# Batched matmul, fp32 in and out: eleven output stores move from GpSimd's software queue to SyncE's hardware queue

## The chip, the cores and the metric

The kernel runs on one core of a Trainium2 chip. The metric is the device time of one launch in microseconds (us). Before the change the median of three runs is 511.96 us (511.52 to 512.17).

## The reference

```python
x:      (32, 512, 1024)  float32
weight: (32, 1024, 768)  float32
out = np.matmul(x, weight).astype(np.float32)      # (32, 512, 768)
```

Inputs are read once (167.77 MB) and the output is written once (50.33 MB). The two operands are cast from fp32 to bf16 on their way into SBUF; products are summed in fp32.

## The kernel before

**Tiling.** The 32 batches are worked on as 16 pairs (`PAIRS`), numbered 0 to 15; pair k holds batches 2k and 2k+1. A pair's x is one transfer (4.19 MB of fp32), its weights are one transfer of 6.29 MB for pairs 2 to 14, and two of 3.15 MB for pairs 0, 1 and 15 (`together`). Its output is one store of 3.15 MB, except for pair 15, whose batches 30 and 31 are stored separately, 1.57 MB each. Output of a pair is collected in a slot of `outs`.

**Buffers.** There are places for the weights of two pairs (`W_SLOTS` 4 batches), for the x of two pairs (`X_SLOTS` 2) and for the output of four pairs (`OUT_SLOTS` 4). Pair a and pair a+4 share an output slot, so the first copy into it for pair a+4 waits for the store of pair a (`slot_free`, on ACT). Pair 15 uses the slot of pair 11.

**Work on a pair.** TensorE (PE) transposes the pair's x in fp32 words (line 173, tile `pt`); VectorE (DVE) spreads each transposed block into `xT` (lines 219, 227). Then PE multiplies: per batch four blocks of rows (`mt`), each with 8 steps over K and two column ranges (lines 165 and 138, tile `pm`). There are two sets of PSUM tiles; each takes two row blocks, then ACT (lines 261, 265) and DVE (lines 270, 272) copy it to `outs`. DVE does the spreading of pair k+1 before its last copy of pair k, so a pair is copied out shortly after the transposes of the next one.

**Loads.** All loads but one are issued by GpSimd (POOL) on its software queue, q0, in program order. The x of pair k+2 waits until the first products of pair k are done (`load_x`, line 111); the weights of pair k+2 wait until pair k is done (`load_w`, line 98; line 102 for single batches). Only the first half of the first x comes over SyncE's queue.

**Stores before.** POOL issues the stores of pairs 0 to 13 on the same queue q0 (`store`, line 119), two at a time in every second turn of its loop, between the load of x and the load of weights; those of pairs 11, 12 and 13 follow all loads. A store waits until the pair is copied out (`copied`). SyncE (SP) passes on the landings of loads to PE (`landed`, signals `s_xr` and `s_wr`), and at its end issues the store of pair 14 and the two of pair 15 on its hardware queue, q1.

Of the kernel before, what the change touches and what calls it, by code (L numbers as in the profile page):

```python
# [12 lines left out]
def kernel(  # L13
# [7 lines left out]
    B, M, K = x.shape  # L21
# [8 lines left out]
    PAIRS = B // 2  # L30
    HELD = 2
    GROUPS = 2 * MT
    W_SLOTS, X_SLOTS, OUT_SLOTS = 4, 2, 4

    pe, dve, act, pool, sp = nc.tensor, nc.vector, nc.scalar, nc.gpsimd, nc.sync
# [25 lines left out]
    def sem(name):  # L61
        sems.append(nc.alloc_semaphore(name))
        return sems[-1]
# [6 lines left out]
    s_free = sem("s_free")  # L70
    s_a, s_ap, s_d, s_dp = sem("s_a"), sem("s_ap"), sem("s_d"), sem("s_dp")
    s_st = [sem(f"s_st{i}") for i in range(OUT_SLOTS)]
    s_fin = sem("s_fin")


# [14 lines left out]
    def together(b):  # L90
        return W_SLOTS <= b < B - 2

    def load_w(b):
        if together(b):
            if b % 2 == 0:
                pool.wait_ge(s_mm, mm_done(b + 1 - W_SLOTS))
                slots = all_ws[:, b // 2 % 2].rearrange("p r ko n -> p r (ko n)")
                pool.dma_start(out=slots, in_=w_two_view[b // 2]).then_inc(s_w[b % W_SLOTS], 16)  # L98
            return
        if b >= W_SLOTS:  # L100
            pool.wait_ge(s_mm, mm_done(b - W_SLOTS))
        pool.dma_start(out=ws[b % W_SLOTS], in_=w_view[b]).then_inc(s_w[b % W_SLOTS], 16)  # L102

    def loads_of_w(b):

        return sum(not (together(i) and i % 2) for i in range(b % W_SLOTS, b + 1, W_SLOTS))

    def load_x(k):
        if k >= X_SLOTS:
            pool.wait_ge(s_mm, mm_begun(k - X_SLOTS))  # L110
        pool.dma_start(out=xs[k % X_SLOTS], in_=x_view[k]).then_inc(s_x[k % X_SLOTS], 16)  # L111

    def copied(eng, j):
        eng.wait_ge(s_ap, j + 1)
        eng.wait_ge(s_dp, j + 1)

    def store(eng, a, sem):
        copied(eng, 4 * a + 3)
        eng.dma_start(out=two_view[a], in_=outs[a % OUT_SLOTS]).then_inc(sem, 16)  # L119

    def store_one(b):
        copied(sp, 2 * b + 1)
        sp.dma_start(out=one_view[b], in_=last_out(b)).then_inc(s_fin, 16)
# [211 lines left out]
    def landed(eng, slot, n, ready, uses=1):  # L335

        eng.wait_ge(slot, 16 * n).then_inc(ready, uses)

    def on_pool():
        pool.dma_start(out=xs[0][:, MT:], in_=x_view[0, :, MT:]).then_inc(s_rest, 16)  # L340
        load_w(0)
        pool.memset(ident, 0.0).then_inc(s_zero, 1)  # L342
        pool.wait_ge(s_zero, 1)
        pool.affine_select(  # L344
            out=ident,
            in_=ident,
            compare_op=mybir.AluOpType.not_equal,
            fill=1.0,
            base=0,
            pattern=[[-1, P]],  # L350
            channel_multiplier=1,
        ).then_inc(s_ident, 1)
        load_w(1)
        load_x(1)
        load_w(2)
        load_w(3)
        def stores(first, last):
            for a in range(max(first, 0), last):
                store(pool, a, s_st[a % OUT_SLOTS])


        for k in range(PAIRS - 2):
            load_x(k + 2)
            if k % 2 == 0:
                stores(k - 3, k - 1)
            load_w(2 * k + 4)
            load_w(2 * k + 5)
        stores(PAIRS - 3 - HELD, PAIRS - 2)

    def on_sp():  # L370
        for b in range(B):
            if b == 0:
                sp.wait_ge(s_cast, 2).then_inc(s_xr, 1)
            elif b % 2 == 0:
                k = b // 2
                landed(sp, s_x[k % X_SLOTS], (k + 1) // X_SLOTS, s_xr)
            if not (together(b) and b % 2):
                landed(sp, s_w[b % W_SLOTS], loads_of_w(b), s_wr, 1 + together(b))
        store(sp, PAIRS - 2, s_fin)
        store_one(B - 2)  # L380
        store_one(B - 1)
        sp.sem_inc(s_zero, 1)

    def clear_on_pool():

        for i, s in enumerate(s_st):
            pool.wait_ge(s, 16 * len(range(i, PAIRS - 2, OUT_SLOTS)))
        pool.wait_ge(s_zero, 2)
        used = range(sems[0].num, s_fin.num)
        pool.dma_reset(used)  # L390
        pool.sem_clear(used)
        pool.wait_ge(s_fin, 48).then_inc(s_fin, -48)

    sp.dma_start(x_first, x_view[0, :, :MT])
    with tc.tile_critical(sync_engine=mybir.EngineType.Activation, no_gpsimd_drain=True):  # L395
        on_pool()
        tc.wait_critical_data_deps()
        on_pe()
        on_dve()
        on_act()  # L400
        on_sp()
        clear_on_pool()
# [30 lines left out]
```

## Time and profile before

| | |
|---|---|
| Median of 3 runs | 511.96 us |
| Span of the profiled execution | 509.6 us |
| Its own time beside the span | not listed apart; the median stands 2.4 us over this span |
| PE busy | 429.4 us (84%) |
| DVE, ACT, POOL busy | 211.7, 114.1, 29.6 us |
| Queue q0 (POOL's, software) | 126.88 MB at the SBUF side, 96.8% of the time of 16 engines |
| Queue q1 (SP's, hardware) | 8.39 MB, 4.0% |
| Mean granted PE clock | 0.947 |

How to read the lines below. A row of a group or a wait names engine, line and operation, then output <- input by the program's names. In the waits, "A <- B: 103.4, 6, 19.2" says that A waited for B for 103.4 us in 6 times, at most 19.2. In a timeline the first two numbers are start and duration in us from the start of the span, and a bracket gives the idle time before and what ended it. In a table of stretches the columns are: the stretch, its length, busy time and count of PE, PEld (weight loads into PE), DVE, ACT and POOL, the granted PE clock, the busy share of the 16 DMA engines, and GB/s. GB/s and MB of a queue count the SBUF side, where a loaded value has 2 bytes and a stored one 4.

### The profile page before, as it was taken

To read this page: it belongs to the slowest core of one execution; us is meant where nothing else is said; L and a number is where in the kernel's file an instruction comes from. 1 tells how busy PE (TensorE), PEld (TensorE's weight loads), DVE (VectorE), ACT (ScalarE), POOL (GpSimd) and SP (SyncE) were. 2 spreads that over 40 slices of the span, in tenths; PEclk is the share of its full clock that TensorE was granted. 3 is DMA by queue.
4 is the path that set the end of the run, shared out by engine and by line. 5 is a ranking of instruction groups with operands and counts; after the bars stand their busy time and mean duration, and the time that the engine had idled before them with its cause. 6 is when DMAs were issued, how large, how long until landed. Compare 5 with 4: busy or idle time off the path is not lost. (4 is left out here: it accounts for less than half of the span.)

```text
span 509.6 us, 5832 instructions
## 1 busy us (share of the span) xinstructions
PE 429.4 (84%) x2560; PEld 172.8 (34%) x1536; DVE 211.7 (42%) x330; ACT 114.1 (22%) x195; POOL 29.6 (6%) x55
## 2 busy tenths in 40 slices
PE   0899989999899399993999949999399994999990
PEld 0525342443325034250343513434034341433420
DVE  1436362454635136351373514635146351454631
ACT  1131312223130231302313023230231302223230
POOL 3000000000101001010010100100001000100000
PEclk9999998999999799996999979999699997999996
DMA  8999999999999999999999999999999999999998
GB/s 262 216 211 216 225 207 221 215 305 247 221 212 230 432 234 214 217 237 432 226 215 217 247 433 216 218 217 259 420 217 217 219 267 408 218 215 229 432 430 347
DMA packets 9299, 135.29 MB, mean 266 GB/s; under 512 B 848, under 2 KB 848, under 8 KB 848
## 3 DMA queue, kind: packets, MB, share of 16 engines
q0 software_dynamic: 8720, 126.88, 96.8%
q1 hardware_dynamic: 576, 8.39, 4.0%
q14 instruction: 3, 0.02, 0.0%
HBM read 167.77 MB, written 50.33 MB: 428 GB/s over the span
## 5 line engine op out<-in xcount | busy, mean ns | idle before, releaser
L165 PE MATMUL pm<-w,xT 128*128 x1024 | 346.2, 389 | 42.0 <-DVE outs L270 38.7
L138 PE MATMUL pm<-w,xT 128*128 x1024 | 284.7, 278 | 0.0
L165 PEld LDWEIGHTS pm<-w,xT 128*128 128x128 bf16 x1024 | 102.3, 100 | 282.8 <-issue 241.0
L270 DVE COPY outs<-pm 64x512 f32<-64x512 f32 x128 | 88.2, 689 | 207.7 <-DVEq L268 206.3
L261 ACT COPY outs<-pm 64x512 f32<-64x512 f32 x128 | 74.2, 580 | 272.6 <-PE pm L138 168.4
L173 PE MATMUL pt<-ident,x 128*128 128x128 f32 x512 | 84.5, 307 | 24.8 <-PEq L177 14.5
L219 DVE COPY xT<-pt 128x1024 bf16<-128x1024 bf16 x120 | 77.7, 687 | 63.9 <-PE pt L173 63.6
L173 PEld LDWEIGHTS pt<-ident,x 128*128 128x128 f32 x512 | 71.2, 210 | 40.0 <-DVE xT L219 18.8
L265 ACT COPY outs<-pm 64x512 f32<-64x512 f32 x64 | 37.0, 579 | 99.5 <-PE pm L138 99.3
L272 DVE COPY outs<-pm 64x512 f32<-64x512 f32 x64 | 43.9, 686 | 0.0
L98 POOL DMA_DIRECT2D w<-in_weight_dram x13 | 9.2, 708 | 264.6 <-PE pm L138 264.6
L111 POOL DMA_DIRECT2D x<-in_x_dram x15 | 8.4, 557 | 123.2 <-PE pm L138 92.4
L119 POOL DMA_DIRECT2D out_dram<-outs x14 | 7.5, 539 | 7.1 <-DVE outs L272 7.1
L227 DVE COPY xT<-pt 128x512 bf16<-128x512 bf16 x16 | 5.7, 418 | 4.1 <-PE pt L173 4.1
L280 DVE CAST x<-outs 128x1024 bf16<-128x1024 f32 x2 | 1.3, 692 | 11.0 <-DMA outs<-in_x_dram 11.0
L102 POOL DMA_DIRECT2D w<-in_weight_dram x6 | 3.2, 544 | 26.5 <-PE pm L138 26.3
L280 ACT ACT_TABLE_LOAD x1 | 1.3, 1283 | 10.7 <-DMA outs<-in_x_dram 10.7
L280 ACT CAST x<-outs 128x1024 bf16<-128x1024 f32 x2 | 2.0, 1042 | 0.0
L340 POOL DMA_DIRECT2D x<-in_x_dram x1 | 0.7, 670 | 0.8 <-POOLq L417 0.8
L344 POOL TENSOR_SCALAR_AFFINE_SELECT ident<-ident 128x128 f32<-128x128 f32 x1 | 0.3, 284 | 0.2 <-POOL ident L342 0.2
L342 POOL MEMSET ident<- 128x128 f32 x1 | 0.2, 232 | 0.0
L417 POOL MEMSET const-float32-0.0<- 128x1 f32 x1 | 0.1, 99 | 0.2 <-issue 0.2
(3 smaller groups left out, 0.3 us busy)
## 6 DMA issues: line engine op xcount, KB each, us to landing
out_dram<-outs POOLq DMA_DIRECT2D x14, 3072.0 KB, 40.1
w<-in_weight_dram POOLq DMA_DIRECT2D x13, 3072.0 KB, 32.9
x<-in_x_dram POOLq DMA_DIRECT2D x15, 2048.0 KB, 34.3
w<-in_weight_dram POOLq DMA_DIRECT2D x6, 1536.0 KB, 30.5
out_dram<-outs SPq DMA_DIRECT2D x1, 3072.0 KB, 18.7
out_dram<-outs SPq DMA_DIRECT2D x2, 1536.0 KB, 13.6
outs<-in_x_dram SPq DMA_DIRECT2D x1, 2048.0 KB, 9.7
x<-in_x_dram POOLq DMA_DIRECT2D x1, 1024.0 KB, 11.6
```

Of the source, the lines that this page charges most:

```text
L98: pool.dma_start(out=slots, in_=w_two_view[b // 2]).then_inc(s_w[b % W_SLOTS], 16)
L111: pool.dma_start(out=xs[k % X_SLOTS], in_=x_view[k]).then_inc(s_x[k % X_SLOTS], 16)
L119: eng.dma_start(out=two_view[a], in_=outs[a % OUT_SLOTS]).then_inc(sem, 16)
L138: return pe.add_instruction(mybir.InstMatmult(name=nc.get_next_instruction_name(), engine=mybir.EngineType.PE, ins=[pe.lower_ap(moving), p ...
L165: last = pe.matmul(*args, start=(ko == 0), stop=(ko == KT - 1))
L173: last = pe.transpose(pts[g % 2][:, j, :], words[:, mo, j::JT], ident)
L219: return dve.tensor_copy(both[g // 2][:, :, :, g % 2].rearrange("p b j i r -> p j b i r"), pt)
L227: last = dve.tensor_copy(rows, pt[:, :, b])
L261: last = act.copy(*piece)
L265: act.copy(*pieces(b, p, 2)[0]).then_inc(s_ap, 1)
L270: last = dve.tensor_copy(*piece)
L272: dve.tensor_copy(*pieces(b, p, 2)[1]).then_inc(s_dp, 1)
```

## The change

SP issues the stores of pairs 0 to 10 inside its loop over batches: after the weights of pair a+1 have landed and been passed on, it waits for pair a's copies and issues its store on q1. The store of pair 11 is issued by SP when batch 30's weights have landed. The stores of pairs 12 and 13 stay with POOL after all loads, each with a semaphore of its own, and the waits at the very end follow.

```diff
+    s_late, s_last = sem("s_late"), sem("s_last")
...
-        def stores(first, last):
-            for a in range(max(first, 0), last):
-                store(pool, a, s_st[a % OUT_SLOTS])
-
-
         for k in range(PAIRS - 2):
             load_x(k + 2)
-            if k % 2 == 0:
-                stores(k - 3, k - 1)
             load_w(2 * k + 4)
             load_w(2 * k + 5)
-        stores(PAIRS - 3 - HELD, PAIRS - 2)
+        store(pool, PAIRS - 4, s_late)
+        store(pool, PAIRS - 3, s_last)
 
     def on_sp():
+        late = PAIRS - 3 - HELD
         for b in range(B):
...
                 landed(sp, s_w[b % W_SLOTS], loads_of_w(b), s_wr, 1 + together(b))
+            if b % 2 and 2 < b < 2 * late + 2:
+                store(sp, b // 2 - 1, s_st[(b // 2 - 1) % OUT_SLOTS])
+            elif b == B - 2:
+                store(sp, late, s_st[late % OUT_SLOTS])
         store(sp, PAIRS - 2, s_fin)
...
-            pool.wait_ge(s, 16 * len(range(i, PAIRS - 2, OUT_SLOTS)))
+            pool.wait_ge(s, 16 * len(range(i, PAIRS - 4, OUT_SLOTS)))
+        pool.wait_ge(s_late, 16)
+        pool.wait_ge(s_last, 16)
```

## Prediction

> **What bounds the kernel now.** I read the queue totals of the page first, then the waits, then the clock and transfer rate by stretch, then the starts of the last pairs on the PE in order of time.
>
> ```profile
> PE 429.4 (84%) x2560; PEld 172.8 (34%) x1536; DVE 211.7 (42%) x330; ACT 114.1 (22%) x195; POOL 29.6 (6%) x55
> q0 software_dynamic: 8720, 126.88, 96.8%
> HBM read 167.77 MB, written 50.33 MB: 428 GB/s over the span
> ACT outs L261 <- DMA out_dram<-outs: 103.4, 6, 19.2
> PE pm L165 <- DVE outs L270: 38.7, 5, 8.2
> 230.00:240.00 10.00, 1.98 (x7) 0.41 (x3) 1.98 (x3) 2.81 (x5) 0.00 (x0) 0.68 1.00 433
> 270.00:280.00 10.00, 10.00 (x63) 3.04 (x31) 3.97 (x6) 3.47 (x6) 0.00 (x0) 1.00 1.02 217
> ```
>
> The kernel moves 167.77 MB in and 50.33 MB out, and POOL's queue alone keeps the 16 engines busy for 96.8% of the span. The two stretches give the rates. While stores run, 433 GB/s; while loads run, 217 GB/s as counted in bf16 at the SBUF side, which is 434 GB/s of fp32 read. Both kinds cost the same per fp32 byte, and the transfers are what bounds the whole. The waits tell something else: ACT waits six times for a store to empty a slot of `outs`, and the PE behind it loses 38.7 us in five stalls. It is tempting to count those 38.7 us as the gain, because early stores remove that wait. But in the stretch 230 to 240, where the PE is busy for 1.98 us of 10, the transfers run at 1.00. The PE stalls cost nothing at the end as long as the queues never run dry.
>
> So I need the rate over a whole cycle, and then the one place where the PE does matter: the last pairs.
>
> ```profile
> 238.35 0.59 PE L165 MATMUL pm<-w,xT 128*128 x1 [8.02 <-DVE outs L270]
> 301.57 0.58 PE L165 MATMUL pm<-w,xT 128*128 x1 [7.27 <-DVE outs L270]
> 364.63 0.58 PE L165 MATMUL pm<-w,xT 128*128 x1 [7.99 <-DVE outs L270]
> 427.80 0.59 PE L165 MATMUL pm<-w,xT 128*128 x1 [7.22 <-DVE outs L270]
> 426.06 1.17 ACT L261 COPY outs<-pm 64x512 f32<-64x512 f32 x2 [18.26 <-DMA out_dram<-outs]
> 386.13 0.39 PE L165 MATMUL pm<-w,xT 128*128 x1
> 406.94 0.52 PE L173 MATMUL pt<-ident,x 128*128 128x128 f32 x3
> 412.62 0.38 PE L165 MATMUL pm<-w,xT 128*128 x1
> 448.45 0.39 PE L165 MATMUL pm<-w,xT 128*128 x1
> 475.20 0.38 PE L165 MATMUL pm<-w,xT 128*128 x1
> ```
>
> The first four rows end the same stall of pairs 7, 9, 11 and 13, so two pairs take (427.80 - 238.35) / 3 = 63.15 us. A pair moves 4.19 MB of x, 6.29 MB of weights and 3.15 MB of output, 13.63 MB; two pairs in 63.15 us are 431.7 GB/s. One pair costs the transfers 31.57 us, of which a store is 7.29 us and the loads 24.3 us. The other rows start pairs 12, 13, 14 and 15 at 386.13, 412.62, 448.45 and 475.20, with the transposes of pair 13 at 406.94. An undisturbed pair thus takes the PE 20.8 us of products and 26.49 us from start to start (26.75 us into the last). The PE needs 26.5 us where the transfers need 31.6 us with a store and 24.3 us without one.
>
> **The change part by part.** Eleven stores leave POOL's queue for SyncE's.
>
> On SyncE (SP), before: the one early load, then stores of pair 14 and of the last two batches.
>
> ```order
> L394 DMA outs<-in_x_dram 128x4096
> L428 UNCONDITIONAL_BRANCH [waits DMAHW0_49,Activation_sequencer_49]
> L119 DMA out_dram<-outs 128x6144 [waits s_cast,s_w0,s_w1,s_x1,s_w2,s_w3,s_x0,s_dp,s_ap]
> L123 DMA out_dram<-outs 128x3072 [waits s_dp,s_ap] x2
> L395 UNCONDITIONAL_BRANCH
> ```
>
> After, the end of SP's list: stores of pairs 9, 10, 11, 14, then the last two batches (s_x and s_w are landings of x and weights, s_dp and s_ap the copies out).
>
> ```order
> L120 DMA out_dram<-outs 128x6144 [waits s_x0,s_w0,s_dp,s_ap]
> L120 DMA out_dram<-outs 128x6144 [waits s_x1,s_w2,s_dp,s_ap]
> L120 DMA out_dram<-outs 128x6144 [waits s_x0,s_w0,s_x1,s_w2,s_dp,s_ap]
> L120 DMA out_dram<-outs 128x6144 [waits s_w3,s_dp,s_ap]
> L124 DMA out_dram<-outs 128x3072 [waits s_dp,s_ap] x2
> L397 UNCONDITIONAL_BRANCH
> ```
>
> A store of pair a now stands behind the landing of pair a+1's weights and behind its own copies. On POOL before, from the x of pair 13 on:
>
> ```order
> L111 DMA x1<-in_x_dram 128x8192 [waits s_mm]
> L98 DMA w<-in_weight_dram 128x2x6144 [waits s_mm]
> L111 DMA x0<-in_x_dram 128x8192 [waits s_mm]
> L119 DMA out_0_dram<-outs 128x6144 [waits s_dp,s_ap] x2
> L98 DMA w<-in_weight_dram 128x2x6144 [waits s_mm]
> L111 DMA x1<-in_x_dram 128x8192 [waits s_mm]
> L102 DMA w<-in_weight_dram 128x6144 [waits s_mm] x2
> L119 DMA out_0_dram<-outs 128x6144 [waits s_dp,s_ap] x3
> ```
>
> And after, from the same x on:
>
> ```order
> L112 DMA x1<-in_x_dram 128x8192 [waits s_mm]
> L99 DMA w<-in_weight_dram 128x2x6144 [waits s_mm]
> L112 DMA x0<-in_x_dram 128x8192 [waits s_mm]
> L99 DMA w<-in_weight_dram 128x2x6144 [waits s_mm]
> L112 DMA x1<-in_x_dram 128x8192 [waits s_mm]
> L103 DMA w<-in_weight_dram 128x6144 [waits s_mm] x2
> L120 DMA out_0_dram<-outs 128x6144 [waits s_dp,s_ap] x2
> ```
>
> The two stores between x and weights of pair 14 are gone from there, and no load waits in a queue behind a store any more.
>
> *The stalls for slots.* All five go: store a is issued near the landing of pair a+1's weights and its slot is wanted three pairs later. Late next is the weight load. Loads and a store run side by side and share the engines, so a pair's weights come every 31.57 us, and the PE waits for each of them. Nothing of the 38.7 us is gained; it is spread over the pairs. POOL's issues (about half a microsecond each) were hidden and stay so. SP's eleven new waits hold back only SP's next signals, for loads that land later than the store they wait beside (x of the pair after next); price nothing.
>
> *The last four pairs.* Before, by the slot wait that ended at 426.06, the queue had moved x of 15 pairs, weights of 14 and 10 stores, 182.4 MB. After, pair 12 can start when x of 13 pairs, weights of 13 and all 11 early stores are through: 170.9 MB. That is 11.5 MB less, 26.7 us at 431.7 GB/s, so pair 12 starts at 399.4. From there no store runs until pair 11's, loads need 24.3 us a pair, and the PE runs free: pairs 13, 14 and 15 start 26.49, 26.49 and 26.75 us apart, at 479.1 for pair 15 against 475.20 now. Batch 30's weights land near 399.4 + 2 x 24.3 + 9.7 + 7.3 = 465; the store of pair 11, issued then beside the last weights, is down 14.6 us and a fixed part later, about 482. The first copy that needs its slot is due a quarter of 20.8 us after pair 15's start, so that wait costs nothing.
>
> *The clock.* The price of waiting for weights shows in pairs with a stall:
>
> ```profile
> 70.00:80.00 10.00, 7.72 (x37) 4.30 (x31) 6.54 (x11) 0.00 (x0) 0.00 (x0) 0.83 0.97 207
> 76.31 0.39 PE L165 MATMUL pm<-w,xT 128*128 x1 [1.75 <-PEq L177]
> 98.79 1.12 PE L173 MATMUL pt<-ident,x 128*128 128x128 f32 x8
> 132.61 0.39 PE L165 MATMUL pm<-w,xT 128*128 x1 [1.50 <-PEq L177]
> 153.42 0.76 PE L173 MATMUL pt<-ident,x 128*128 128x128 f32 x5
> 222.36 0.38 PE L165 MATMUL pm<-w,xT 128*128 x1
> 254.03 0.65 PE L173 MATMUL pt<-ident,x 128*128 128x128 f32 x4
> ```
>
> After a gap of 1.75 us pair 2 takes 22.48 us (granted clock 0.83 in that stretch), 1.7 us over 20.8. After 1.50 us pair 4 takes 20.81, nothing over. Pair 7, with 8.02 us of stall inside, takes 31.67 - 8.02 = 23.65, so 2.8 us over. In the changed kernel pair 12 starts after a wait of 31.57 - 26.49 = 5.1 us, or 3.1 us if pair 11 itself started slow. Bounds 0 and 2.8; I take 2.0, between the two stalled rows and nearer the shorter gap. For pairs 2 to 11 it is hidden in the wait. For pair 12 it isn't, since nothing behind it waits for loads. Pair 15 then starts at 481.1, 5.9 us later than now.
>
> The Trainium skill, "TensorE: Matmul & The Clock Gate", in the table of why this matters, asks for no idle gap over about 3 us between bursts of matmuls; it speaks against this change. The 1.75 us row shows a slower clock already below that.
>
> *The end.*
>
> ```profile
> 0.74 0.38 SPq L394 DMA_DIRECT2D outs<-in_x_dram  x1
> x<-in_x_dram POOLq DMA_DIRECT2D x1, 1024.0 KB, 11.6
> 1.26 0.67 POOL L340 DMA_DIRECT2D x<-in_x_dram  x1 [0.81 <-POOLq L417]
> 488.04 10.72 SPq L123 DMA_DIRECT2D out_dram<-outs  x2
> DMA to landing us min/median/max: 10.2/37.0/51.8
> ```
>
> The last store is now issued near 488.04 + 10.72 - 0.33 = 498.4 and, as the shortest of all, lands 10.2 us later at 508.6, with others still in flight beside it. After: issued at 498.4 + 5.9 = 504.3, with the rest nearly done. Alone it moves 1.57 MB in 3.6 us plus a fixed part. The first two loads bound that part: both together are 4.19 MB, 9.7 us, and are down at 1.26 + 11.6 = 12.9, which leaves 12.9 - 9.7 - 0.74 = 2.4 us. It lands at 510.4, 1.8 us later than before. The span goes from 509.6 to 511.4; the median of the runs shown, 511.96, stands 2.4 us over the span, which I keep: **513.8 us**. All the transfers alone would end where they do now, so this is a gap at the end in which only the last store runs.
>
> **The rivals.**
>
> *Mixed traffic is slower.* The trace has no stretch in which stores of one queue run beside loads of the other. Eleven stores, each shared for 14.6 us, are 160 us; 1% off the rate there delays pair 12 and so the end by 1.6 us. The lowest rate seen with both queues at work is here:
>
> ```profile
> 490.00:500.00 10.00, 6.16 (x38) 1.76 (x18) 3.97 (x6) 2.32 (x4) 0.00 (x0) 0.99 0.98 421
> ```
>
> Against 433 that is 2.8%, 4.5 us on top: 518.3 us. For it: nothing has shown such a mixture at full rate. Against: the cycle of 63.15 us, with four changes of direction, already reaches 431.7. The other bound is a gain of 0.3%, the 433 of stores alone, 0.5 us.
>
> *Pair 12 starts at full clock.* If its wait falls so that the clock is not lowered, pair 15 starts at 479.1, the last store is issued at 502.3 and would land at 508.4; the transfers together still end at 508.6, so 512.0 us, the same. For it: 1.50 us cost nothing. Against: 1.75 us did. By the skill's rule above, pairs would alternate: a full-clock pair leaves 5.1 us of wait, the next, slow, leaves 3.1 us, about at its limit.
>
> *Faster.* Loads no longer stand behind stores and two queues feed each engine; if that lifts the mixed rate above 431.7 GB/s, pair 12 and the total come 1.6 us earlier per 1%. With pair 12 at full clock this decides from 0.7% on; at 1.5% it gives 509.6 us. Against: stores alone and loads alone both stop at 433 to 434, as if at one limit. The Trainium skill, "DMA: Bandwidth & Descriptors", rules for kernel authors, says spreading transfers over issuing engines does not help, as they interleave on the same 16 engines; no run here shows it yet.
>
> **How the numbers follow.** A run of this kernel can be told from no change from about 0.2%, 1.0 us. Forecast, slower by about 2 us: 0.46. Mixed traffic slower: 0.27. Full clock at pair 12, same: 0.18. Faster: 0.09. Slower together 0.73. The range runs from 511.2, which leaves out the faster cases, to 518.5, the lowest mixed rate seen.
>
> **What would show it.** Right: no ACT wait for stores, PE waits of 3 to 5 us before pairs 2 to 12, clock below 1 after them, pair 12 starting near 399 and pair 15 near 481, the last store landing alone in about 6 us. Wrong: pair 12 starting after 401 (the rate), PE stalls in pairs 13 to 15 (loads issued too late), a span under 508.6, or a rate in the shared stretches clearly off 432.

## The result and the profile after

The changed kernel takes 513.98 us (513.38 to 514.30, 5 runs) against 511.60 us (511.34 to 512.17, 5 runs) on the same chip: a ratio of 1.0042, 95% interval 1.0031 to 1.0053. By that ratio it is slower by 2.1 us (1.6 to 2.7); the two medians lie 2.4 us apart. The forecast was 513.8 us.

Totals and queues of the profile's page after, the PE's waits for weights, and one stretch of 210 us from the table of stretches, first after, then before:

```profile
PE 430.9 (84%) x2512; PEld 174.6 (34%) x1536; DVE 211.6 (41%) x330; ACT 114.4 (22%) x195; POOL 23.1 (5%) x43
q0 software_dynamic: 6992, 89.13, 79.1%
q1 hardware_dynamic: 2304, 46.14, 21.3%
HBM read 167.77 MB, written 50.33 MB: 426 GB/s over the span
PE pm L139 <- PEq L178: 41.6, 9, 9.8
PE pm L139 <- DVE outs L271: 4.5, 2, 2.3
190.00:400.00 210.00, 178.41 (x1036) 72.94 (x638) 89.63 (x137) 45.64 (x79) 8.26 (x13) 0.93 1.01 265
```

```profile
190.00:400.00 210.00, 182.00 (x1079) 73.38 (x651) 89.71 (x137) 46.14 (x81) 13.14 (x22) 0.93 1.02 261
```

No wait of ACT for a store is left in the waits after; it was 103.4 us. In its place stand nine waits of the PE for a signal of SP (`PEq L178`), 41.6 us, about what the five stalls had cost. Two more, 4.5 us together, stand before pairs 5 and 9, put down to the DVE; with them the PE waits before each of pairs 2 to 12. The longest, 9.8 us, is that of pair 2, whose weights land at 84.0 us where they landed at 75.9. The busy share of the DMA engines hardly moves: 1.01 where it was 1.02.

Starts on the PE after, in order of time: products of pairs 6, 10, 11 and 12, the transposes behind pair 12, and products of pairs 13, 14 and 15.

```profile
211.17 0.42 PE L139 MATMUL pm<-w,xT 128*128 x1 [5.31 <-PEq L178]
337.39 0.42 PE L139 MATMUL pm<-w,xT 128*128 x1 [5.30 <-PEq L178]
369.26 0.42 PE L139 MATMUL pm<-w,xT 128*128 x1 [3.52 <-PEq L178]
400.82 0.42 PE L139 MATMUL pm<-w,xT 128*128 x1 [3.77 <-PEq L178]
424.03 0.52 PE L174 MATMUL pt<-ident,x 128*128 128x128 f32 x3
429.92 0.27 PE L139 MATMUL pm<-w,xT 128*128 x1
456.55 0.27 PE L139 MATMUL pm<-w,xT 128*128 x1 [0.20 <-DVE xT L220]
483.29 0.27 PE L139 MATMUL pm<-w,xT 128*128 x1
```

In this trace the very first product of a pair is often missing, so the row shown is the second. The two stand 0.22 us apart at full clock (386.13 and 386.35 before) and 0.40 us at half clock (400.48 and 400.88 in the run `s11pool_again` below), so a start is that much ahead of the row and the wait in its bracket that much shorter. Four pairs take 337.39 - 211.17 = 126.22 us, 31.56 us each. Pair 12, at half clock, starts near 400.4, where it started at 386.13 before; behind it nothing waits, and pair 15 starts at 483.1, where it was 475.20.

Stores after, their first and last issue and the shortest way from issue to landing (the tile `out_dram`), and the last stretch; then the last stretch before:

```profile
L124 SPq DMA_DIRECT2D out_dram<-outs x2: 332/332/332, 495.9 to 506.3; - x2
DMA to landing us min/median/max: 5.1/19.6/40.3
500.00:512.30 12.30, 4.04 (x26) 1.08 (x11) 3.01 (x5) 1.74 (x3) 0.00 (x0) 0.85 0.64 272
```

```profile
500.00:509.60 9.60, 0.00 (x0) 0.00 (x0) 0.00 (x0) 0.00 (x0) 0.00 (x0) 0.50 0.77 326
```

The last store is issued at 506.3 instead of 498.4 and lands 5.1 us later, at 511.4 instead of 508.6. The DMA engines are busy for 0.64 of the time from 500 on, where it was 0.77 before, and the PE still works there for 4.04 us, where it had ended before: too little is left to move beside the last store.

### The profile page after: what moved, and what is told of

Same layout as the page of the kernel before. It is cut to its first block, busy times and chain, and to the rows that moved or that the text cites. A ratio compares the mean times of both kernels' runs of the same rounds, so it can differ in the third digit from the quotient of the medians.

```text
span 512.3 us, 5785 instructions
## 1 busy us (share of the span) xinstructions
PE 430.9 (84%) x2512; PEld 174.6 (34%) x1536; DVE 211.6 (41%) x330; ACT 114.4 (22%) x195; POOL 23.1 (5%) x43
## 5 line engine op out<-in xcount | busy, mean ns | idle before, releaser
L166 PE MATMUL pm<-w,xT 128*128 x976 | 336.6, 394 | 0.0
L139 PE MATMUL pm<-w,xT 128*128 x1024 | 288.0, 281 | 48.3 <-PEq L178 41.6
L120 POOL DMA_DIRECT2D out_dram<-outs x2 | 1.1, 536 | 7.7 <-DVE outs L273 7.6
```

The lines of the kernel that those rows point to most:

```text
L139: return pe.add_instruction(mybir.InstMatmult(name=nc.get_next_instruction_name(), engine=mybir.EngineType.PE, ins=[pe.lower_ap(moving), p ...
L166: last = pe.matmul(*args, start=(ko == 0), stop=(ko == KT - 1))
```

## The experiments

Each kernel was compared with runs of the kernel before on its own chip; the ratio is to those. Theory: early stores stand ahead of pair 12's weights, the PE therefore starts its last four pairs late, and with the lowered clock at pair 12 it ends behind the transfers. Rivals: loads and stores mixed from two queues are slower; the even spacing itself costs; the place of pair 11's store costs.

**Stores two pairs later** (`later2`), the mixture kept:

```diff
-            if b % 2 and 2 < b < 2 * late + 2:
-                store(sp, b // 2 - 1, s_st[(b // 2 - 1) % OUT_SLOTS])
+            if b % 2 and 2 + 2 * 2 < b < 2 * late + 2 + 2 * 2:
+                store(sp, b // 2 - 1 - 2, s_st[(b // 2 - 1 - 2) % OUT_SLOTS])
```

> The changed kernel, with each of the stores of pairs 0 to 10 issued by SyncE two pairs later (pair a's when the weights of pair a+3 have landed); queue, mixture with loads, pair 11's store and the end are as in the changed kernel. Theory (the early stores stand ahead of pair 12's weights, so the PE starts its last four pairs too late and ends last): two stores of 7.3 us fewer before pair 12, which starts near 385 instead of 401; time back to the kernel before, 511.6 us within 0.5. Rival (stores of the hardware queue beside loads of the software queue run slower): as many stores are mixed, so the time stays near 514.

Measured 512.31 us against 511.83, ratio 1.0010 (1.0000 to 1.0019). Pairs 12 and 15 on the PE, and the stores:

```profile
385.69 0.38 PE L139 MATMUL pm<-w,xT 128*128 x1 [3.45 <-PEq L178]
478.20 0.27 PE L139 MATMUL pm<-w,xT 128*128 x1
L124 SPq DMA_DIRECT2D out_dram<-outs x2: 332/332/333, 490.8 to 501.2; - x2
DMA to landing us min/median/max: 8.1/19.6/55.0
```

As many stores are mixed with loads, the PE waits and its clock drops as often, and most of the loss is gone. What counts is which transfers stand ahead of pair 12.

**Stores one pair later** (`later1`): the same edit with `2 * 1` for `2 * 2` and `- 1 - 1` for `- 1 - 2`.

> The changed kernel with each of the stores of pairs 0 to 10 one pair later. Theory: ten early stores instead of eleven stand ahead of pair 12, which starts near 393.5; it waits for pair 13's weights again, so the gain at pair 15 is about 2 us (481), the last store is issued near 503.5 and the transfers end as late as it does: 512.3 us within 0.5, like two pairs later. If each pair earlier costs the same (a rate, not an end), the time is midway between 512.3 and 514.0 or above.

512.26 us against 511.67, ratio 1.0008 (0.9999 to 1.0016): the same as two pairs later, as expected, so the loss is not a fixed amount per pair; it has a point from which it begins.

**One store per turn on the software queue** (`pool1`, `pool1_again`), the kernel before with:

```diff
-            if k % 2 == 0:
-                stores(k - 3, k - 1)
+            stores(k - 2, min(k, PAIRS - 4) - 1)
```

> The kernel before, with its stores of pairs 0 to 10 one in every turn of POOL's loop (pair a in turn a+2) instead of two in every second turn: all on the software queue, nothing mixed, but spread evenly like those of the changed kernel. Theory: pair 12 starts near 385 after nine stores, the PE waits about 5 us for weights in each pair and runs at a lower clock after it, and the end does not move: 511.6 us within 0.5. Rival (the even spacing, with a wait and a lower clock in every pair, is what costs): near 514.

> One store in every turn on the software queue, once more. In its first profile pair 15 started at 478.6 and the last store was issued at 501.7, early enough, and yet all landings at the end came 2 us late, with 3 us between the first and the last of the 16 engines for one load (1 us before). If that spread is of this order of stores on one queue, both the time near 513.7 and the spread return; if it was of that chip or that run, the time goes to 512.

513.70 us against 511.83, ratio 1.0041 (1.0028 to 1.0055); again 513.89 against 511.67, 1.0040 (1.0026 to 1.0053). The expectation of 511.6 us failed here. In the first profile, pairs 12 and 15 and the stores:

```profile
386.97 0.42 PE L138 MATMUL pm<-w,xT 128*128 x1 [3.49 <-PEq L177]
478.64 0.27 PE L138 MATMUL pm<-w,xT 128*128 x1
L123 SPq DMA_DIRECT2D out_dram<-outs x2: 332/332/333, 491.3 to 501.7; - x2
DMA to landing us min/median/max: 8.9/43.1/53.7
```

The PE is early enough, as in `later2`, and yet the last store, issued at 501.7, lands at 510.6. What differs shows in the 16 increments that each transfer makes as its engines finish. For batch 30's weights, first and last engine in us from the start of the span:

```
before        463.6   464.7
after         464.6   465.8
later2        464.4   465.1
pool1         463.6   466.5
pool1_again   463.5   467.2
```

In `pool1` and `pool1_again` the first engine is where it is in the kernel before, and the last is 2.9 and 3.7 us behind it; in the other three kernels it is 0.7 to 1.2 us behind. In `pool1` the spread is 0.4 us in the beginning, 0.7 us near 195 us, as in the kernel before, and grows from about 250 us on. So the rival isn't borne out as worded either: `later2` has the same even spacing, with SP's queue, and neither the spread nor the loss. Stores alternating singly with loads on the one software queue let engines fall behind. Why, and which engine, was not tried; it stays open.

**Full clock at pair 12** (`warm12`):

```diff
+    WARM_AT, WARM = 12, 14
...
+            with pe.If_eq(pair, WARM_AT):
+                pe.wait_ge(s_a, 1)
+                pe.wait_ge(s_d, 1)
+                for i in range(WARM):
+                    pe.matmul(pms[0][0], xs[0][:, 0, :P], xs[0][:, 0, :512], start=True, stop=True)
             w_pair = all_ws[:, bass.ds(nc.snap(odd, min_val=0, max_val=1), 1)]
...
+            pe.reg_add(pair, pair, 1)
```

> The changed kernel, with 14 products of 128x512 on the PE, whose results are overwritten, between the transposes and the products of pair 12 alone. They fill about 3 us of its wait of 3.8 us, so the clock should stay up. Theory: pair 12 takes 20.8 us instead of 23.4, pair 15 starts near 480.7, the last store is out 2.5 us earlier and the time falls to about 511.8 us. Rival (rate of the transfers, or the stores at the end): pair 15 starts earlier but the time stays near 514. If the clock is not held by them: nothing changes, 514.

512.57 us against 511.83, ratio 1.0017 (1.0008 to 1.0026), 0.8 us above the 511.8 expected. The added products (one of the 14 has no record), pair 12, the transposes behind it, pair 15, the clock around pair 12, and the stores; then that stretch in the changed kernel:

```profile
397.00 2.97 PE L210 MATMUL pm<-x 128*128 128x512 bf16 x13
400.18 0.39 PE L167 MATMUL pm<-w,xT 128*128 x1 [0.21 <-issue]
420.99 0.52 PE L175 MATMUL pt<-ident,x 128*128 128x128 f32 x3
480.64 0.39 PE L167 MATMUL pm<-w,xT 128*128 x1
396.00:410.00 14.00, 13.69 (x80) 5.04 (x51) 5.40 (x9) 2.90 (x5) 0.56 (x1) 1.00 1.03 219
L125 SPq DMA_DIRECT2D out_dram<-outs x2: 332/332/332, 493.5 to 503.9; - x2
DMA to landing us min/median/max: 5.4/19.5/45.0
```

```profile
396.00:410.00 14.00, 10.22 (x49) 3.42 (x29) 4.71 (x8) 1.74 (x3) 0.56 (x1) 0.76 1.03 220
```

The clock is 1.00 where it was 0.76, pair 12 takes 20.8 us instead of 23.6 (from 400.4 to 424.03), and the last store leaves 2.4 us earlier. Its landing improves by 2.1 us, to 509.3, and no further. The ratio falls from 1.0042 in the first comparison; against the changed kernel's second run below (1.0032) the intervals overlap, so the size in time is less sure than in the trace.

**Pair 11's store on POOL** (`s11pool`, then `s11pool_again` beside `again`, the changed kernel):

```diff
+            if a == PAIRS - 1:
+                act.wait_ge(s_pool, 16).then_inc(s_free, 1)
...
+        store(pool, PAIRS - 5, s_pool)
         store(pool, PAIRS - 4, s_late)
...
-            elif b == B - 2:
-                store(sp, late, s_st[late % OUT_SLOTS])
```

> The changed kernel with pair 11's store back on POOL, first after all loads, as in the kernel before. Theory: it decides nothing, since its slot is wanted only some microseconds after it lands either way: 514.0 us within 0.5. Rival (the store of pair 11 beside the last weights delays the end): back towards 511.6.

> The kernel with pair 11's store on POOL after all loads, once more. In its first profile pair 12 started at full clock, which by the theory alone explains its 512.85 us. If the place of that store matters by itself, it is again 1 us or more faster than the changed kernel beside it, and its profile shows it also where pair 12 starts slow; if not, the two agree within 0.5 us where the clock does.

> The changed kernel once more, as the measure for the next three on the same chip. The clock before pair 12 is lowered in the first profile; where a run meets it at full clock, the theory gives 512.3 us, else 514.0.

The first time 512.85 against 511.83, ratio 1.0019 (1.0010 to 1.0028), which looked like an effect. Side by side it is none: 513.27 us, 1.0029 (1.0020 to 1.0038), and `again` 513.23 us, 1.0032 (1.0020 to 1.0044), both against 511.82. The start of pair 12 in the two profiles of this variant, and the transposes behind it:

```profile
400.50 0.27 PE L140 MATMUL pm<-w,xT 128*128 x1 [2.18 <-DVE outs L275]
421.08 1.13 PE L175 MATMUL pt<-ident,x 128*128 128x128 f32 x8
```

```profile
400.48 0.61 PE L167 MATMUL pm<-w,xT 128*128 x1 [3.26 <-PEq L179]
424.21 0.40 PE L175 MATMUL pt<-ident,x 128*128 128x128 f32 x2
```

One execution met pair 12 at full clock (20.8 us with the first product, which has no row there), the other not (23.7 us). The same kernel does both.

**The PE held for 3 us at pair 14** (`hold_after`, `hold_before`): the edit of `warm12` with `WARM_AT` 14 for 12, in the changed kernel and in the kernel before.

> The changed kernel with 14 products of 128x512, about 3.0 us, ahead of pair 14's products on the PE, where nothing waits (their results are overwritten). Theory (the PE's last four pairs set the end): all of it shows, 517.0 us. Rival (transfers set the end): nothing or under 1 us shows.

> The same 14 products ahead of pair 14 in the kernel before. Theory: there the last store is issued 10.2 us before it lands and would need about 6, so about 4 us of delay are covered: 511.8 us within 0.5. Rival (the PE sets the end there as well): 514.8.

In the changed kernel 516.94 us against 511.82, ratio 1.0102 (1.0086 to 1.0117), 3.7 us over `again`; between the two profiles the issue of the last store and its landing both move by 2.8 us. In the kernel before 512.71 us, 1.0013 (1.0004 to 1.0022), 0.9 us more, above what was expected. But the median span is 509.9 us against 509.8: inside the span the delay is covered, and what makes up the rest outside it isn't shown. Stores of the first, then of the second:

```profile
L125 SPq DMA_DIRECT2D out_dram<-outs x2: 332/332/332, 497.7 to 508.1; - x2
DMA to landing us min/median/max: 5.1/19.6/39.5
```

```profile
L124 SPq DMA_DIRECT2D out_dram<-outs x2: 332/332/332, 491.6 to 502.0; - x2
DMA to landing us min/median/max: 6.9/36.6/49.7
```

Put in order, the profiles of these kernels give one curve (issue of the last store and its landing, us from the start of the span):

| kernel | issued | landed |
|---|---|---|
| before | 498.4 | 508.6 |
| later2 | 501.2 | 509.3 |
| hold_before | 502.0 | 508.9 |
| later1 | 502.8 | 509.6 |
| s11pool (full clock at pair 12) | 503.4 | 509.3 |
| warm12 | 503.9 | 509.3 |
| again | 505.3 | 510.4 |
| after | 506.3 | 511.4 |
| s11pool_again | 506.5 | 511.6 |
| hold_after | 508.1 | 513.2 |
| *pool1* | 501.7 | 510.6 |

Up to about 504 the transfers end near 509 (508.6 to 509.6) whenever the last store is issued; from 505 on it needs 5.1 us alone, and each microsecond of the PE is one of the end. `pool1` lies off the curve because its engines ended apart.

## Why the prediction was right, and where it was off

*The stalls gain nothing.* Right: 38.7 us of stalls became 46.1 us of waits for weights by the rows, and the time did not fall. The waits were to be 3 to 5 us; pair 2's was over 9.

*The spacing.* Worked out 31.57 us a pair, measured 31.56. The rival of a slower mixture is refuted at its size of 1% and more. A small remainder is there: with the PE early enough (`later1`, `later2`, `warm12`), the transfers end at 509.3 to 509.6, 0.7 us or more after those of before, where the forecast had nothing. The landings of batch 30's weights, 464.4 in `later2` against 463.6 for the first engine, with the same bytes ahead of them, show that it has arisen before the end; what makes it isn't shown. The Trainium skill, "DMA: Bandwidth & Descriptors", rules for kernel authors, holds that spreading over issuing engines does not help bandwidth, since all transfers interleave on the same engines. These spacings agree. `pool1` beside `later2`, both with one store per pair, shows that the queue is still not indifferent.

*The last four pairs.* Right as a mechanism, shown by moving the stores (`later1`, `later2`) and by holding the PE (`hold_after`, `hold_before`). Of its terms, pair 12's start was put at 399.4 and came at 400.4; the clock was put at 2.0 us and cost 23.6 - 20.8 = 2.8 us in this trace, the upper of its bounds, and 22.5 - 20.8 = 1.7 us in the profile of `again` (400.55 to 423.04). Pair 15 started at 483.1, not 481.1, and the last store left 7.9 us later than before, not 5.9.

*The end.* The fixed part of the last store was taken at 2.4 us, a bound from two first loads that share the start. It is 5.1 - 3.6 = 1.5 us. This error offset half of the one before: the landing moved by 2.8 us where 1.8 was worked out. Two choices of base helped as well. The 2.4 us from span to time compared a median with the span of one execution; in the five runs of the changed kernel the time stands 2.0 to 2.1 us over its own span. And the forecast rose from a median of three runs, 511.96; that of five is 511.60. So the forecast rise was 1.8 us and the medians rose by 2.4, and the profiled span, that of the slowest of the five runs, by 2.7: that 513.8 lies within 0.2 us of 513.98 is in part luck.

*The clock's rival* (pair 12 at full clock, same as before) was seen in one profile of `s11pool`, not in the changed kernel itself: in both of its profiles the clock is down in pair 12. Nor do its pairs alternate: in the first profile nine of eleven run slow. The length of a wait alone does not decide. In one execution of `hold_after` two pairs began after nearly the same wait, and the ten microseconds from there have a clock of 0.83 in one and 1.00 in the other:

```profile
147.56 0.39 PE L167 MATMUL pm<-w,xT 128*128 x1 [2.15 <-DVE outs L280]
273.78 0.39 PE L167 MATMUL pm<-w,xT 128*128 x1 [2.12 <-PEq L179]
147.50:157.50 10.00, 9.94 (x51) 2.81 (x26) 2.65 (x5) 1.99 (x4) 0.56 (x1) 0.83 1.02 274
273.70:283.70 10.00, 9.92 (x61) 3.03 (x31) 2.70 (x5) 2.90 (x5) 0.56 (x1) 1.00 1.01 275
```

Over all these profiles, waits up to 1.66 us before a pair's products cost no clock, all from 2.7 us on did, and those between went either way. The Trainium skill, "TensorE: Matmul & The Clock Gate", Part 1, describes the clock's window of about 3.4 us as free-running: by that, the phase decides along with the length, and these traces agree. In the clock records of each profile, the slow stretches start on one grid of 3.41 us through the whole execution, and all but the one running at its end last one, two or three steps of it. From 60 to 495 us, each of the 110 falls follows a step in which the records have the PE busy for at most 1.66 of 3.41 us; of the steps that kept full clock, the least busy had 1.17. So neither the length nor this share draws a sharp line. The Trainium skill's table of why this matters, on the same page, has a figure of about 3 us for a harmless wait; that is too long here, by the 1.75 us row.

## What to carry to other kernels

Where transfers bound a kernel as here, an earlier store saves nothing; it takes the place of a load that the compute engine will need. Hold stores back for the time behind the last loads, and work out two things at the end: when the transfers would be done by themselves, and when the last store can be issued. The slack between the two (here about 5 us before the change) is what a reordering may use up; beyond it each microsecond of the compute engine counts in full.

## What was not expected of the hardware

One store per turn on the software queue, with nothing else changed, costs 2 us: the first of the 16 engines keeps its time and the last falls 2.9 and 3.7 us behind, in the two profiles. With SP's queue and the same spacing the spread is 0.7 us (`later2`). And a wait of 1.7 to 2.7 us may lower the PE clock or not, even within one execution; the falls lie on a grid of 3.41 us.
